# Attention and output projection: the merge weighed ahead of a pair's last values, and the projection's first column tile computed inside the last merge

## The chip, the cores and the metric

The kernel runs on one core of one Trainium2 chip. A core has five engines with a queue each: TensorE (PE in the profile; its weight loads are the row PEld), VectorE (DVE), ScalarE (ACT), GpSimd (POOL) and SyncE (SP), which here only issues DMAs. The metric is the device time of one execution in microseconds. The kernel before was timed in three runs: 2714.69, 2719.62 and 2720.20 us, so its median is 2719.62 us.

## What is computed

One layer of a decoder for 2048 prompt tokens and 64 sample tokens, with a model width of 1024. The first half of the mixer is attention with 8 heads of 64, in three patterns of window and dilation whose outputs are merged with weights from their softmax denominators. The second half is a gated linear attention. Both halves, side by side, go through the output projection `w_o`. A feed-forward part follows. Cut to what the change touches:

```python
PATTERNS = ((128, 1), (512, 4), (2048, 16))

def combine_patterns(results):
    outs = jnp.stack([o for o, _ in results], axis=0)
    lses = jnp.stack([l for _, l in results], axis=0)
    w = jax.nn.softmax(lses, axis=0)
    return jnp.sum(w[..., None] * outs, axis=0)

def prompt_attn(q, k, v):
    return combine_patterns([dilated_prompt(q, k, v, w, d) for w, d in PATTERNS])
...
mixed = jnp.concatenate([o_a.reshape(B, T, -1), o_b.reshape(B, T, -1)], axis=-1) @ w_o
x = x + rmsnorm(mixed, g_post_mix)
```

## The kernel before

**Stages.** `run` calls `sweeps` (projections and gated linear attention), `attention` (prompt attention), and `tail` (output projection, norms, feed-forward). The order in each engine's queue is not the order of the program: a planner simulates the engines and moves instructions that are ready ahead of others, and the code ties it down where it matters with `after(b, a)` (b is queued behind a on the same engine, without a wait) and `line`, which chains instructions that way one after the other.

**Attention.** The 8 heads are taken in four pairs (`pr` 0 to 3). A pair has three patterns, and a pattern four groups `g`. A group is cut into two units for the first two patterns and one for the third, so a pair has 20 units (`AtUnit`). A unit has three steps. `qk_` makes the scores of both heads on TensorE (L1880, tile `pas`), adds the mask and takes the row minimum of the negated scores on VectorE (L1885), and exponentiates on ScalarE (L1889). The minima and sums go into small tables `ML` (tile `aml`). `t` transposes the probabilities on TensorE (L1906, `pat`) and evicts them (`apt`, L63 on ScalarE, L65 on VectorE). `pv` multiplies them with the values (L1925, `pao`) and evicts the outputs unweighted into `OP` (`aop`, L65). Units wait in `fifo`: `pv` of a unit is issued two to three units behind its scores, and units are taken out in twos. For the second and third pattern GpSimd gathers the strided queries first (`at_gather`, L1134, `aqg`). PSUM has eight banks: four for scores (tag `as`), two for the transposes (`apt`), two for outputs (`ao`).

**Merge.** When a pair's last unit has been taken out of the fifo, `drain` makes a generator `at_merge` for it, and the loop over the next pair takes it forward by `next(pend)`, as often per group as the table `mst` says. The generator's first part weighs the patterns: 16 products on TensorE bring two of the `ML` tables into the order of the third (L1143 and L1146, `pam`), VectorE picks and reduces (L1152 to L1161, `atm`, `aw`), and some 15 small operations with one exponential on ScalarE (L1175) give the weights `aaw`. For pairs 0 to 2 the second step transposes `aaw` on TensorE (L1201, `pab`), sends it through DRAM (`awd`) so that it can be loaded spread over 64 rows (`awb`), and GpSimd then multiplies and adds the outputs (L1214 to L1221) and stores the merged rows to DRAM (`mixa`).

**Last merge.** For pair 3 nothing follows that would hide it, so it is done from PSUM, in four blocks `cb` of 128 columns by four residues. Of a block, each of the three patterns needs its weights spread (L1237 on ScalarE or L1239 on GpSimd, by the list `aa`), four transposes on TensorE (L1241, `pab`) and one multiplication on VectorE (L1242). Then two additions follow (L1245, L1247) and the store. The small operations of the weights are on GpSimd for this pair.

**Output projection.** It computes eight column tiles `m` for each of four token chunks `c` of 528 tokens. A column tile sums over eight input tiles `k`, in the order `WORD = (4, 5, 6, 7, 0, 1, 2, 3)`: 4 to 7 come from the linear attention (`mixb`), 0 to 3 from pairs 0 to 3 of the attention (`mixa`). Every operand is split into a high part (ScalarE, L70) and a low part (VectorE, L73), and three products with two halves of the tokens each are taken (L1439, `pbo`), so an input tile costs a column tile six products. `wo_pre` loads and splits the first column tile's weights and the input tiles 4, 5 and 6 during pair 3, in memory that no longer serves the attention. The other input tiles of chunk 0 (7, 0, 1, 2) are loaded and split by `wo_x(0)` at the start of `tail`, input tile 3 is split inside the last merge, straight from its result. `wo(0)` first takes column tiles 0, 1 and 2 through the input tiles 4 to 2, then adds input tile 3. The tail has its own PSUM pool of eight banks (`g1`).

## Time and profile before

| | |
|---|---|
| median of three runs | 2719.62 us (2714.69 to 2720.20) |
| the profiled execution | 2722.77 us, span 2721.0 us, mean granted clock 0.992 |
| attention, from first to last score and value product | about 765 to 1035 us of the span |
| last merge and start of the projection | about 1035 to 1062 us |
| TensorE busy in 1062 to 1252 us (rest of the projection) | 190.00 of 190 us |

All other numbers are read from one profiled execution. Its time is the span plus what lies around it, and it is 3.15 us above the median of the runs. A row of the timeline gives the start in us from the span's start, the busy time, the engine, the line of the kernel, the operation, output and inputs by tile name, shapes, and how many neighbouring instructions were put together; in brackets stands the idle time ahead of it and who ended it. A row of the waits gives who waited for whom. "Granted clock" is the share of TensorE's full clock that it was allowed.

### The profile page before, as it was taken

Reading aid. Unit: us, or ns where it says so; the run is one execution under the profiler, and the core shown is the slowest. Engines: PE = TensorE matmul, PEld = TensorE weight load, DVE = VectorE, ACT = ScalarE, POOL = GpSimd, SP = SyncE. Lnnn points to the kernel's source line nnn. Section 1 sums busy time; section 2 is a strip of 40 time slices with the busy share of each in tenths; the row PEclk is TensorE's granted clock in tenths of the full one; section 3 lists DMA queues with packets and bytes.
Section 4 is the critical chain, followed back from the end, with each engine's and each line's share of the span. In section 5 each row is a group of like instructions: output and inputs, shape, how many; then the busy total and the mean of one; then the engine's idle time right before and its main releaser. Section 6 shows DMA issues by size and latency. Waiting matters only on the chain.

```text
span 2721.0 us, 58225 instructions
## 1 busy us (share of the span) xinstructions
PE 2643.1 (97%) x22203; PEld 2518.3 (93%) x22203; DVE 1853.8 (68%) x4441; ACT 1270.2 (47%) x2961; POOL 373.6 (14%) x516
## 2 busy tenths in 40 slices
PE   8999999999999998999999999999999999999998
PEld 6888899878798887999999999999999999999998
DVE  7645645555457785468799899865776665766666
ACT  6535433333368883445555445433344332443333
POOL 2223120000045672011000020000110000200001
PEclk9999999999999998999999999999999999999999
DMA  8755536799776663376687589985798865976654
GB/s 321 255 176 179 186 131 211 268 331 369 272 263 191 192 173 109 129 260 251 244 286 288 196 314 333 350 294 198 256 330 289 282 228 203 336 248 216 221 184 164
DMA packets 288935, 661.67 MB, mean 243 GB/s; under 512 B 33344, under 2 KB 83136, under 8 KB 286608
## 3 DMA queue, kind: packets, MB, share of 16 engines
q1 hardware_dynamic: 260368, 588.97, 62.9%
q0 software_dynamic: 11296, 37.12, 3.7%
q10 hardware_dynamic: 16992, 31.86, 3.2%
q8 instruction: 175, 2.87, 0.4%
q14 instruction: 104, 0.85, 0.1%
HBM read 511.45 MB, written 146.37 MB: 242 GB/s over the span
## 4 chain that ended last, share of the span: by engine, by line
PE 79%; DVE 8%; DMA 6%; ACT 2%; issue 2%; POOL 1%; SPq 1%; DVEq 0%; ACTq 0%; POOLq 0%
PE pfd L92 17%; PE pv L399 9%; PE pq L92 8%; PE pfe L1636 8%; PE pfd L1636 8%; PE pfa L1636 7%; PE pbo L1439 7%; PE pfb L1636 4%; PE pas L1880 2%; DVE ws L73 2%; PE pao L1925 2%; PE pat L1906 2%; DMA raw<-in_xn 1%; DMA wr<-in_wd 1%; DMA ws<-d_wst 1%
## 5 line engine op out<-in xcount | busy, mean ns | idle before, releaser
L70 ACT ACTIVATE ws<-wr 128x512 fp32r<-128x512 f32 (+1 forms) x482 | 292.7, 616 | 423.7 <-PE pfd L92 160.9
L92 PE MATMUL pfd<-hh,ws 128*128 128x264 f32 x2816 | 470.2, 285 | 5.0 <-ACT ws L70 3.8
L73 DVE TENSOR_TENSOR ws<-wr,ws 128x512 fp32r<-128x512 f32 (+1 forms) x482 | 319.8, 669 | 127.5 <-ACT ws L70 116.1
L92 PEld LDWEIGHTS pfd<-hh,ws 128*128 128x128 f32 x2816 | 397.3, 188 | 6.5 <-ACT ws L70 4.8
L92 PE MATMUL pfd<-hl,ws 128*128 128x264 f32 x1408 | 298.6, 284 | 0.0
L1636 PE MATMUL pfe<-xh,ws 128*128 128x264 f32 x1496 | 290.5, 286 | 7.7 <-DVE u L1623 4.8
L1636 PE MATMUL pfa<-xh,ws 128*128 128x264 f32 x1496 | 289.8, 285 | 6.2 <-ACT ws L70 3.5
L1636 PE MATMUL pfd<-xh,ws 128*128 128x264 f32 x1408 | 288.9, 285 | 0.5 <-DVE gt L1623 0.3
L1636 PEld LDWEIGHTS pfe<-xh,ws 128*128 128x128 f32 x1496 | 236.4, 189 | 9.6 <-DVE u L1623 5.7
L1636 PEld LDWEIGHTS pfa<-xh,ws 128*128 128x128 f32 x1496 | 235.3, 188 | 8.3 <-ACT ws L70 4.6
L399 PE MATMUL pv<-wh,xh 128*128 128x256 f32 (+1 forms) x816 | 233.2, 286 | 2.2 <-DVE th L696 2.2
L1636 PEld LDWEIGHTS pfd<-xh,ws 128*128 128x128 f32 x1408 | 231.2, 189 | 0.9 <-DVE gt L1623 0.5
L399 PE MATMUL pv<-wl,xh 128*128 128x256 f32 (+1 forms) x816 | 231.3, 283 | 0.0
L399 PE MATMUL pv<-wh,xl 128*128 128x256 f32 (+1 forms) x816 | 231.2, 283 | 0.0
L92 PEld LDWEIGHTS pfd<-hl,ws 128*128 128x128 f32 x1408 | 223.6, 188 | 0.0
L1636 PE MATMUL pfd<-xl,ws 128*128 128x264 f32 x704 | 200.5, 285 | 0.0
L1665 DVE TENSOR_TENSOR acc<-acc,pfd 128x264 f32<-128x264 f32 x304 | 116.9, 424 | 115.9 <-PE pfd L92 115.2
L1889 ACT ACTIVATE ass<-ass,aml 128x256 f32<-128x256 f32 (+1 forms) x384 | 172.7, 453 | 46.1 <-DVE aml L1885 45.6
L92 PE MATMUL pq<-xh,wh 128*128 128x512 f32 (+2 forms) x480 | 173.2, 367 | 8.3 <-ACT xh L234 7.9
L1636 PE MATMUL pfe<-xl,ws 128*128 128x264 f32 x616 | 175.6, 285 | 0.0
L1636 PE MATMUL pfa<-xl,ws 128*128 128x264 f32 x616 | 175.0, 284 | 0.0
L92 PE MATMUL pq<-xh,wl 128*128 128x512 f32 (+2 forms) x480 | 173.0, 361 | 0.0
(334 smaller groups left out, 6277.3 us busy)
## 6 DMA issues: line engine op xcount, KB each, us to landing
ws<-d_wst SPq DMA_DIRECT2D x248, 512.0 KB, 5.4
wr<-in_wu SPq DMA_DIRECT2D x114, 512.0 KB, 4.8
d_wst<-ws SPq DMA_DIRECT2D x88, 512.0 KB, 3.6
wr<-in_wd SPq DMA_DIRECT2D x160, 256.0 KB, 3.5
wr<-in_wt SPq DMA_DIRECT2D x60, 512.0 KB, 8.0
wh<-d_wbs SPq DMA_DIRECT2D x35, 512.0 KB, 5.4
wl<-d_wbs SPq DMA_DIRECT2D x35, 512.0 KB, 5.4
skp<-in_ckt SPq DMA_DIRECT2D x16, 1024.0 KB, 9.0
```

Of the source, the lines that this page charges most:

```text
L70: h = nc.scalar.activation(hi, src, AF.Copy)
L73: return h, (nc.gpsimd if lo_eng == "p" else nc.vector).tensor_tensor(lo, src, hi.bitcast(F32), op=ALU.subtract)
L92: mm = nc.tensor.matmul(o, ww[:, k, :], xx[:, s0:s0 + n], start=(k == order[0] and i == 0), stop=(k == order[-1] and i == 2))
L399: mm = nc.tensor.matmul(ps[:m, :256], x[:, t0:t0 + m], w[:, k % 4, :], start=(k == 0 and i == 0), stop=(k == KT - 1 and i == 2))
L1439: self.lastmm = nc.tensor.matmul(o, ww[:, k, :], xx[:, s0:s0 + n], start=k == self.WORD[0] and i == 0, stop=k == self.WORD[-1] and i == 2)
L1636: self.lastmm = nc.tensor.matmul(bank[:, :H], w[:, ww, k, :], xx, start=new and k == 0 and j == 0, stop=k == 3 and j == 2, skip_group_chec ...
L1665: nc.vector.tensor_tensor(acc[m][:, s0:s0 + n], acc[m][:, s0:s0 + n], pz, op=ALU.add)
L1880: self.line(nc.tensor.matmul(ps[:, sc:sc + nk], lq, rk[z], start=(z == 0), stop=(z == 1)))
L1889: ex = nc.scalar.activation(ssb[:, sc:sc + nk], ssb[:, sc:sc + nk], AF.Exp, bias=self.ml[:, idx, h:h + 1], scale=-1.0, accum_out=self.ml[: ...
L1906: self.line(nc.tensor.transpose(ptp[:, len(tl), :], ssb[:, sc + 128 * j:sc + 128 * j + 128], L.ident))
L1925: self.line(nc.tensor.matmul(po[64 * h:64 * h + 64, blk, :], L.vq[self.base + kb][:, 64 * h:64 * h + 64], pt[:, j, :], start=st, stop=sp))
```

## The change

**The merge is made earlier.** In `drain`, when the last unit of a pair is the next to be taken out, the transposes of that unit are issued first if the fifo is being emptied, the merge is made and its first part is issued at once, ahead of the value products of the last two units. The table `mst` gives one step less in the second group. The `pam` products of pair 3 take their bank from the scores' tag, and the small operations of its weights go to VectorE.

**The last merge is interleaved with the projection.** `attention` now starts `wo(0)`. Four times it takes one step of the projection's column tile 0 (first input tiles 4 to 7, then 0, 1, 2), and one block of the merge. The blocks use only the `ao` banks for their transposes. Two of three spreads go to ScalarE and one to GpSimd. Both additions of a block go to GpSimd. The 16 columns of block 1 that chunk 0 needs are added on VectorE beforehand.

**Loads and buffers.** `wo_pre` loads the first weights in two halves, and then seven of the eight input tiles instead of three. The memory at the right side holds 16 split input tiles instead of 8 and no raw weights; four raw weight tiles and the split weights of column tiles 1 and 2 now lie at the left, behind 16 tiles that are placed first. The attention's PSUM pool stays open for the tail, whose banks go round the same eight by the tags `as`, `as`, `apt`, `ao`.

```diff
-    AB = dict(mst=((1, 1, 2, 1, 1, 1, 0, 1, 0, 0, 1, 1), (1, 1, 2, 1, 1, 1, 1, 1, 0, 1, 1, 1)),
+    AB = dict(mst=((1, 0, 2, 1, 1, 1, 0, 1, 0, 0, 1, 1), (1, 0, 2, 1, 1, 1, 1, 1, 0, 1, 1, 1)),
...
-            self.app = self.pool(ctx, "atp", bass.MemoryType.PSUM)
+            self.app = self.pool(self.tctx, "atp", bass.MemoryType.PSUM)
+            self.psum, self.bi = self, 0
...
                     un.t()
-                    un.pv()
-                    if un.last:
+                    if fifo and fifo[0].last:
+                        end = fifo[0]
+                        if not n:
+                            end.t()
                         for _ in pend or ():
                             pass
-                        pend = self.at_merge(un.pr, un.ML, un.OP)
+                        pend = self.at_merge(end.pr, end.ML, end.OP)
+                        next(pend)
+                    un.pv()
...
             drain(0)
+            self.wog = self.wo(0, self.xnext)
+            for _ in range(4):
+                next(self.wog)
+                next(pend)
             for _ in pend:
                 pass
...
-        pm = pp.tile([128, 512], F32, name=self.n("pam"), tag="ao", bufs=AB["po"])
+        pm = pp.tile([128, 512], F32, name=self.n("pam"), tag="as" if pr == 3 else "ao", bufs=AB["ps" if pr == 3 else "po"])
...
-        em, line = (nc.gpsimd, lambda x: x) if pr == 3 else (nc.vector, self.line)
+        em, line = nc.vector, (lambda x: x) if pr == 3 else self.line
...
-                if j in AB['aa']:
+                if (3 * cb + i) % 3 < 2:
                     nc.scalar.copy(ab, src)
...
                 for r in range(4):
-                    nc.tensor.transpose(pb[:, r, :], W[i][:, r, :], self.ident)
+                    tr = nc.tensor.transpose(pb[:, r, :], W[i][:, r, :], self.ident)
+                    if r == 0 and i == 0:
+                        self.after(tr, self.lastmm)
                 nc.vector.tensor_tensor(OP[i][:, :, sl], OP[i][:, :, sl], pb, op=ALU.mult)
...
+                nc.gpsimd.tensor_tensor(OP[1][:, :, sl], OP[0][:, :, sl], OP[1][:, :, sl], op=add)
+                nc.gpsimd.tensor_tensor(mo.rearrange("p (m r) -> p r m", r=4), OP[1][:, :, sl], OP[2][:, :, sl], op=add)
...
     def bank(self, name):
-        return self.psum.tile([128, 512], F32, name=self.n(name), tag="g1", bufs=8)
+        return self.tile([128, 512], F32, self.n(name))
+
+    def tile(self, shape, dt, name, tag=None, bufs=None):
+        tg, nb = (("as", "ps"), ("as", "ps"), ("apt", "ppt"), ("ao", "po"))[self.bi // 2 % 4]
+        self.bi += 1
+        return self.app.tile(shape, dt, name=name, tag=tg, bufs=self.AB[nb])
...
-        for k in self.WORD[:3]:
+        hi, lo = (self.slot("w", [128, 8, 128], F32R, n) for n in ("wh", "wl"))
+        for j in range(2):
+            ks = slice(4 * j, 4 * j + 4)
+            r = self.raw()[:, :512].rearrange("p (k c) -> p k c", k=4)
+            nc.sync.dma_start(r, a["wo"][0].rearrange("p (k c) -> p k c", k=8)[:, ks])
+            for i, e in zip(self.split(hi[:, ks], lo[:, ks], r, "v"), self.atl):
+                self.after(i, e)
+            yield
+        self.wow.append((hi, lo))
+        for k in self.WORD[:7]:
+            if k == 2:
+                yield
+                yield
...
-        for m in range(3 if c == 0 else 0):
-            part(m, self.WORD[:-1])
+        if c == 0:
+            for ks in (self.WORD[:4], *((k,) for k in self.WORD[4:-1])):
+                part(0, ks)
+                yield
+            for m in (1, 2):
+                part(m, self.WORD[:-1])
```

## The prediction

> **What bounds the kernel now.** I read the page first, then the waits of TensorE over the attention of pairs 1 to 3 and over the hand-over to the output projection (waiting engine, line, what it waited for: us in total, times, longest).

> ```profile
> PE 2643.1 (97%) x22203; PEld 2518.3 (93%) x22203; DVE 1853.8 (68%) x4441; ACT 1270.2 (47%) x2961; POOL 373.6 (14%) x516
> ```
> ```profile
> PE pab L1201 <- DVE aaw L1184: 5.8, 3, 1.9
> PE pas L1880 <- POOL aqg L1134: 2.1, 3, 1.1
> ```
> ```profile
> PE pab L1241 <- ACT awb L1237: 6.3, 1, 6.3
> PE pbo L1439 <- DVE aop L1242: 2.0, 1, 2.0
> PE pbo L1439 <- DVE xl L73: 1.8, 1, 1.8
> ```

> TensorE bounds the whole, so a change pays what it removes from TensorE's idle time or slow time, and nothing else. There are two such places. Each of the three ordinary merges stops TensorE once, 5.8 us together, because the transpose at L1201 needs the finished weights `aaw`. The last merge and the start of the projection stop it for 6.3 + 2.0 + 1.8 = 10.1 us. Both have a second price, which the windows show (columns: length, PE, PEld, DVE, ACT, POOL busy with counts, granted clock, DMA share, GB/s):

> ```profile
> 830.00:844.00 14.00, 12.10 (x132) 11.11 (x130) 13.64 (x60) 11.06 (x40) 0.00 (x0) 1.00 0.67 200
> 840.00:845.00 5.00, 2.83 (x24) 2.42 (x23) 4.30 (x23) 4.36 (x16) 0.00 (x0) 1.00 0.89 297
> 845.00:850.00 5.00, 5.00 (x47) 4.53 (x46) 2.52 (x10) 2.08 (x8) 2.70 (x3) 0.66 0.48 157
> ```
> ```profile
> 830.06 1.97 PE L1925 MATMUL pao<-apt,av 128*64 128x128 f32 x32
> ...
> 833.63 1.00 PE L1143 MATMUL pam<-aml,atab 128*128 128x64 f32 x8
> ...
> 845.42 3.38 PE L1925 MATMUL pao<-apt,av 128*64 128x128 f32 x32
> ```

> In the window with the idle TensorE is busy for 2.83 of 5 us, and in the next the granted clock is 0.66: the same 32 value products take 3.38 us instead of 1.97. So one stop costs 1.92 us of idle (5.8 over three) plus 3.38 - 1.97 = 1.4 us of slow clock, 3.3 us in all; three stops, 10.0 us.

> [...]

> **Part 1: ordinary merges weighed before the last values.** Before, the merge's first part was made only at the end of the next pair's fourth unit, and its `pam` products ran at 833.63, behind the value products of the old pair's last two units (from 830.06). After, it is made ahead of them, so `pam` moves about 833.63 - 830.06 = 3.6 us forward. Nothing is added on TensorE: `pam` and the 32 value products change places. The transpose at L1201 stays at its place in the order. The chain on VectorE that starts behind `pam` therefore has 3.6 us more, and only 1.92 were missing. What speaks against counting all of it is VectorE, busy for 13.64 of the 14 us from 830: the chain gets ahead only by passing evictions and score passes, which then come later themselves. They have room only behind the transpose, where VectorE is busy 2.52 us in 5. I take the idle as gone, 5.8 us. Of the slow clock I take less. GpSimd gathers the strided queries, and TensorE already waits 2.1 us for it (`aqg`, above) in the later pairs, so a faster TensorE meets that wait earlier. I count the clock's 1.4 us whole for one pair, half for the second, none for the third: 2.1. Part 1 is -7.9 us, between -10.0 (everything) and 0 (VectorE gives nothing back).

> **Part 2: the last merge.** Here are the chain of waits, TensorE's timeline, the windows of this stage and of the last pair ahead of it, and the groups of the stage 1035 to 1056:

> ```profile
> 1033.97 0.42 DVE atm L1152
> ...
> 1040.57 0.62 ACT awb L1237
> ...
> 1056.15 18.93 PE pbo L1439 x141
> ```
> ```profile
> 1033.86 1.09 PE L1925 MATMUL pao<-apt,av 128*64 128x128 f32 x14
> 1041.24 8.33 PE L1241 MATMUL pab<-c_ident,awb 128*128 128x128 f32 x48 [6.29 <-ACT awb L1237]
> ```
> ```profile
> 1041.00:1050.00 9.00, 8.52 (x49) 8.28 (x49) 7.16 (x12) 3.10 (x6) 6.92 (x10) 0.66 0.08 30
> 1057.00:1061.00 4.00, 4.00 (x23) 4.00 (x22) 4.00 (x5) 2.27 (x4) 0.00 (x0) 0.57 0.75 253
> 985.00:1000.00 15.00, 13.93 (x144) 12.12 (x140) 13.46 (x43) 14.14 (x51) 14.84 (x12) 1.00 0.81 197
> 1000.00:1020.00 20.00, 18.87 (x190) 17.90 (x189) 13.25 (x79) 18.90 (x80) 19.39 (x18) 0.91 0.31 95
> 1062.00:1252.00 190.00, 190.00 (x1572) 190.00 (x1571) 107.56 (x180) 81.03 (x170) 19.18 (x28) 1.00 0.59 203
> ```
> ```profile
> L1242 DVE TENSOR_TENSOR aop<-aop,pab 128x512 f32<-128x512 f32 x12 | 7.8, 684 | 2.8 <-PE pab L1241 2.8
> L1239 POOL TENSOR_SCALAR awb<-aaw 128x512 f32<-128x512 f32 x7 | 4.2, 616 | 1.4 <-PE pab L1241 1.4
> ...
> L1247 POOL TENSOR_TENSOR amo<-aop,aop 128x512 f32<-128x512 f32 x2 | 2.6, 1284 | 0.7 <-DVE aop L1245 0.5 <-DVE aop L1242 0.2
> L1249 POOL DMA_DIRECT2D d_mixa<-amo x4 | 2.2, 557 | 4.6 <-DVE amo L1247 4.0 <-DVE halo L1365 0.4 <-POOL amo L1247 0.3
> L70 ACT ACTIVATE xh<-br 128x528 fp32r<-128x528 f32 x4 | 2.2, 627 | 0.0
> ```

> What is lost before: 10.1 us idle, the clock in the transposes 9.0 x (1 - 0.66) = 3.1, the clock at 1057 4.0 x (1 - 0.57) = 1.7. Together 14.9 us.

> What is left after, counted from the end of the attention's value products (1033.86 + 1.09 = 1034.95). The chain from `atm` (1033.97) to the first spread weight (1040.57 + 0.62 = 1041.2) lasts 7.2 us. It starts earlier by the 18 value products that now follow `pam` instead of preceding it (18 x 1.97 / 32 = 1.1 us) and by the evictions between them, about 0.8 by estimate: 1.9. Eleven small operations go from GpSimd to VectorE, and three crossings between engines with them; three such operations in the two places:

> ```profile
> 843.67 0.44 DVE L1184 TENSOR_TENSOR aaw<-aaw,amm 128x32 f32<-128x32 f32 x3
> ```
> ```profile
> 1040.05 0.71 POOL L1184 TENSOR_TENSOR aaw<-aaw,amm 128x32 f32<-128x32 f32 x3 [0.47 <-DVE amm L1182]
> ```

> Eleven save 11 x (0.71 - 0.44) / 3 = 1.0, and with the crossings I estimate 1.2 us. So the weight is there 6.3 - 1.9 - 1.2 = 3.2 us behind the value products. TensorE fills this with 24 products of column tile 0, at 18.93 / 141 = 0.134 us each 3.2 us. The stop is covered; were the cover gone (input tiles 4 to 7 not split in time), 3.2 us would come back. Then come four blocks. VectorE has 12 multiplications (7.8), one 512-wide split and small pieces (estimate 1.2), and perhaps part of the two weight splits (estimate 0.5): 9.5 us. TensorE's own work there is 48 transposes, 8.33 x 0.66 = 5.5 us at full clock, and 18 products, 2.4 us: 7.9. So 1.6 us are lost, and I add 0.5 for the entry and 1.4 for GpSimd, whose part per block (spread 0.62, two additions 2 x 1.28, issue 0.56: 3.7 us) is longer than VectorE's. Loss after: 3.5. Part 2 is 3.5 - 14.9 = -11.4 us; bounds of the loss 1 (VectorE alone) and 10 (rival three), so -13.9 to -4.9.

> The waits for `aop` and `xl` go too: the banks stay in the attention's pool, and tiles 7, 0, 1, 2 are split before the merge. Late next are tile 3 and the weights of column tiles 1 and 2. Tile 3 is needed behind 84 products (11.3 us), the weights at the end of the blocks. Their 512 KB loads can start only when the K strips of pair 3 are free, but that is ahead of the last transposes.

> **Part 3: what moves forward.** Four more input splits now run inside pair 3: four loads on SP's queue, 4 x 0.627 = 2.5 us on ScalarE, about as much on VectorE. ScalarE is busy 14.14 of 15 and 18.90 of 20 us there, so they are not free; TensorE however idles there for GpSimd (14.84 of 15, 19.39 of 20). I count +1.5, between 0 and +3. The load of tile 2 is the risky one:

> ```profile
> 1023.17 0.35 SPq L1411 DMA_DIRECT2D br<-d_mixa  x1
> ```

> It waits until GpSimd has stored the second block of pair 2, and what is queued behind it on SP waits too. Its split stands before the last transposes on ScalarE or behind them; wrongly placed it holds up the eviction of the last scores' transposes (in the 3 above). From 1062 to 1252 TensorE is busy for 190.00 of 190 us, so a lead won here is carried on. The rings of the tail keep their number of buffers, and the banks still go round eight; I cost these at nothing, covered by that same full stretch.

> **A rule against the change.** VectorE's split of a weight tile beside GpSimd and without it:

> ```profile
> 989.22 1.91 DVE L73 TENSOR_TENSOR wl<-wr,wh 128x1024 fp32r<-128x1024 f32 x1
> ```
> ```profile
> 1057.87 4.62 DVE L73 TENSOR_TENSOR wl<-wr,wh 128x1024 fp32r<-128x1024 f32 x4
> ```

> With GpSimd at work one takes 1.91 us, alone 4.62 / 4 = 1.16. The change puts eight additions on GpSimd beside VectorE's work. By these rows the two weight splits could lose 2 x 0.75 = 1.5 us, inside the bounds above. [...]

> **Sum.** -7.9 - 11.4 + 1.5 = -17.8 us; I take -17, because the splits may cost some of the pairs' gain twice. The profiled execution took 2722.8 us with a span of 2721.0, the median of the runs is 2719.6, lowest 2714.7: the profiled one lies 3.2 us above the median. From the profiled one 2705.8, from the median 2702.6. I forecast the median: 2703.

> **The rivals.** *VectorE is full (0.22).* The merge chain starts earlier but ends no earlier, or the clock stays low. For it: 13.64 of 14 us. Against: 3.6 us of head start for 1.92 missing. Part 1 falls to about -2: 2719.6 - 2 - 11.4 + 1.5 = 2707.7. [...]

> *GpSimd paces the last merge (0.12).* If its spreads stay behind its additions, a block takes 3.7 us and some 0.5 for TensorE and VectorE's answer, four take 16.8 instead of 9.5: Part 2 falls to 3.5 + 7.3 - 14.9 = -4.1, so 2719.6 - 7.9 - 4.1 + 1.5 = 2709.1. Against is GpSimd's own order in this stage, where the planner put spreads of later blocks ahead of the first addition:

> ```profile
> 1040.72 2.37 POOL L1239 TENSOR_SCALAR awb<-aaw 128x512 f32<-128x512 f32 x4
> ...
> 1045.94 1.29 POOL L1247 TENSOR_TENSOR amo<-aop,aop 128x512 f32<-128x512 f32 x1 [0.25 <-DVE aop L1242]
> ```

> *The change does nothing in the order (0.06).* The planner moves `pam` and the projection back behind the values: some -4 is left, 2716.

> *Slower: `pam` holds an output bank (0.05).* In the ordinary pairs `pam` now takes one of two banks that the value products need. If VectorE, full there, frees it late, TensorE stops ahead of the last unit's values. Up to 1.92 us of stop per pair this only replaces the old one. From about 5 us per pair (5 + 1.4 - 3.3 = 3.1 more, 9.3 over three pairs) it eats the 11.4 - 1.5 us of the rest, and at 8 us per pair, with rival three beside it: 3 x 6.1 - 4.1 + 1.5 = +15.7, 2735. VectorE's two reads of `pam` are 0.42 us each, so this needs a long queue ahead of them.

> **How the numbers follow.** The forecast has 0.55; its own range is 2698 to 2709 (bounds of the two parts). The cases reach 2713 with 1 in 10 beyond, below 2696 lie all bounds at their best: 2696 to 2713. A measurement of this kernel can tell about 0.2%, 5.4 us. Below 2714.2 lie the forecast and the first two rivals but for their ends: 0.87. Within 0.2%: 0.08. Slower: 0.05.

> **What would show it.** Right: no wait of TensorE at the ordinary transposes and a granted clock of 1.00 behind them; `pbo` products between the last merge's transposes; the first wait of the last merge under 1 us; `xl` and the banks gone from TensorE's waits. Wrong: the 1.9 us waits stay or turn into waits for `pao` banks; waits on GpSimd's `awb` in the blocks; a longer `aqg` wait; a late weight split behind the blocks.

## The result and the profile after

| kernel | median | range | runs |
|---|---|---|---|
| before | 2719.62 us | 2714.69 to 2720.20 | 5 |
| after | 2730.64 us | 2728.86 to 2737.67 | 5 |

The changed kernel is slower: ratio 1.0050, 95% interval 1.0034 to 1.0066. The prediction was 2703 us and faster. The profiled execution of after took 2728.86 us, with a span of 2727.1 us and a mean granted clock of 0.989 (before 0.992).

**The ordinary merges.** The waits of TensorE over pairs 1 to 3 (820 to 985 us), in after:

```profile
PE pao L1963 <- DVE apt L65: 6.9, 4, 3.3
PE pam L1152 <- DVE aop L65: 1.0, 1, 1.0
PE pas L1918 <- POOL aqg L1143: 0.6, 1, 0.6
```

The 5.8 us at the transpose are gone, as forecast. Yet the list adds up to 8.5 us. In before it was 8.1: 5.8 at the transpose and 2.3 in three more groups:

```profile
PE pas L1880 <- POOL aqg L1134: 0.9, 2, 0.6
PE pat L1906 <- DVE apt L65: 0.8, 3, 0.3
PE pao L1925 <- ACT apt L63: 0.6, 1, 0.6
```

The idle time has moved. VectorE's timeline at the merges in pairs 2 and 3, both in after, shows the first reason, and GpSimd's timeline in pair 2 shows the stores that VectorE waits for:

```profile
896.70 0.42 DVE L1161 TENSOR_TENSOR atm<-pam,atab 128x256 f32<-128x256 f32 x1 [5.34 <-DMA d_mixa<-amo]
```
```profile
964.17 0.42 DVE L1161 TENSOR_TENSOR atm<-pam,atab 128x256 f32<-128x256 f32 x1 [4.52 <-DMA d_mixa<-amo]
```
```profile
890.00 1.27 POOL L1228 TENSOR_TENSOR aop<-aop,awb 128x512 f32<-128x512 f32 x1 [2.30 <-DMA awb<-d_awd]
891.35 1.29 POOL L1230 TENSOR_TENSOR amo<-aop,aop 128x512 f32<-128x512 f32 x1
892.93 0.58 POOL L1232 DMA_DIRECT2D d_mixa<-amo  x1 [0.30 <-POOL amo L1230]
```

The weighing's table `atm` lies in one of two buffers with the tag `amo`. The other users of that tag are the merged rows, which the older pair's merge is still making on GpSimd and storing. Moved forward, the weighing meets those stores: VectorE stands at `atm` for 5.3 and 4.5 us. The next `apt` copies in its order run only behind `atm` (in pair 2 at 897.38), and TensorE stops for them. A low clock follows (columns as in the prediction):

```profile
895.00:900.00 5.00, 1.47 (x10) 1.07 (x12) 3.30 (x10) 0.00 (x0) 4.00 (x4) 0.70 0.69 207
900.00:905.00 5.00, 5.00 (x34) 4.67 (x30) 4.60 (x19) 3.29 (x11) 0.00 (x0) 0.62 0.69 197
```

In pair 1 no older merge exists. There `atm` waits for `pam` alone (2.1 us), and no such stop follows.

**The last merge.** The `pbo` blocks run between the transposes, and no wait of TensorE there is over 0.7 us. But when the blocks are done TensorE has nothing (its timeline, then SP's):

```profile
1052.87 1.32 PE L1249 MATMUL pab<-c_ident,awb 128*128 128x128 f32 x8
1064.23 0.81 PE L1469 MATMUL pbo<-xh,wh 128*128 128x264 f32 x2 [10.05 <-ACT wh L70]
```
```profile
1029.91 4.19 SPq L1510 DMA_DIRECT2D bx<-in_xn  x3
1055.62 1.27 SPq L1446 DMA_DIRECT2D wx<-d_mixb  x3
1056.94 2.04 SPq L1297 DMA_DIRECT2D wr<-in_wo  x4
```

The raw weights of the next column tiles (`wr`) were issued at 1056.94. From 1034.1 SP stood at `wx`, the first input tiles of the next chunk, whose buffers come free only after GpSimd's last additions. In the program the weights come first, but the planner put `wx` ahead. The chain of waits goes through it:

```profile
1054.33 1.28 POOL aop L1268
1055.61 0.02 issue
1055.62 0.33 SPq L1446
...
1056.94 6.16 DMA wr<-in_wo
1063.10 0.02 issue
1063.13 1.06 ACT wh L70
```

**The end.** From the start of the last `pfd` product to the end of the span before took 14.8 us, after 18.4. The wait there, after and then before:

```profile
PE pn L126 <- DVE fssq L1307: 5.2, 1, 5.2
```
```profile
PE pn L126 <- DVE fssq L1293: 2.5, 2, 1.7
```

**Where the time went.** The table gives stretches in us between starts of the same products, read from the timelines. "s192" is the score product (`pas`) with that number, counted from 0; a pair has 192. "v" is the last value product (`pao`), "p126" a projection product (`pbo`) with that number, which is where three column tiles have had seven input tiles, "d" the last `pfd`. "Before again" is experiment 10 below, the same kernel a second time. The last four columns are experiments 1, 5, 9 and 6. Each column is one execution; that of experiment 1 was the fastest of its runs, that of experiment 5 the slowest.

| stretch | before | before again | after | weights first | + table | + tile 2 | early pairs + table |
|---|---|---|---|---|---|---|---|
| s192 to s264 (merge in pair 1) | 33.2 | 31.6 | 30.8 | 30.8 | 30.8 | 30.8 | 30.8 |
| s384 to s456 (merge in pair 2) | 32.6 | 33.8 | 35.4 | 35.3 | 32.1 | 33.4 | 33.1 |
| s456 to s576 | 33.6 | 33.7 | 32.9 | 33.0 | 35.9 | 33.9 | 35.8 |
| s576 to s648 (merge in pair 3) | 32.5 | 30.9 | 35.0 | 34.8 | 30.6 | 30.7 | 31.8 |
| s648 to v (rest of pair 3) | 48.3 | 50.6 | 50.4 | 50.6 | 52.6 | 47.4 | 51.1 |
| v to p126 (last merge, column tiles) | 36.0 | 34.1 | 37.0 | 28.8 | 28.9 | 27.3 | 37.3 |
| d to the end | 14.8 | 14.7 | 18.4 | 18.5 | 18.5 | 18.5 | 14.7 |

Against the mean of the two traces of before, after loses 2.1 and 3.3 us at the merges in pairs 2 and 3, 1.0 in the rest of pair 3, 2.0 from v to p126 and 3.7 at the end. It gains 1.6 at the merge in pair 1 and 0.8 behind the one in pair 2. Together that is +9.7 us. The spans of the traces differ by less, 6.0 us, because after takes 3.9 us less from p126 to d; there the traces of all kernels lie between 1631 and 1639 us, and why is not shown. The medians of the runs differ by 11.0 us: the profiled execution of before was slower than its median, that of after faster.

### The profile page after: what moved, and what is told of

It reads as the page before. It is cut to its first block, busy times and chain, and to the rows that moved or that the text cites. A ratio compares the mean times of both kernels' runs of the same rounds, so it can differ in the third digit from the quotient of the medians.

```text
span 2727.1 us, 58244 instructions
## 1 busy us (share of the span) xinstructions
PE 2646.7 (97%) x22203; PEld 2519.7 (92%) x22203; DVE 1852.6 (68%) x4449; ACT 1273.9 (47%) x2965; POOL 381.6 (14%) x508
## 4 chain that ended last, share of the span: by engine, by line
PE 78%; DMA 8%; DVE 6%; POOL 3%; issue 2%; ACT 2%; SPq 0%; DVEq 0%; ACTq 0%; POOLq 0%
PE pfd L92 17%; PE pv L399 9%; PE pfe L1674 8%; PE pfa L1674 8%; PE pfd L1674 8%; PE pq L92 7%; PE pbo L1469 7%; PE pfb L1674 4%; DMA raw<-in_xn 2%; DVE ws L73 1%; PE pas L1918 1%; PE pao L1963 1%; PE pat L1944 1%; POOL aqg L1143 1%; POOL aop L1223 1%
## 5 line engine op out<-in xcount | busy, mean ns | idle before, releaser
L70 ACT ACTIVATE ws<-wr 128x512 fp32r<-128x512 f32 (+1 forms) x482 | 293.3, 616 | 411.5 <-PE pfd L92 148.6
L92 PE MATMUL pfd<-hh,ws 128*128 128x264 f32 x2816 | 476.4, 286 | 5.7 <-DVE up L1661 4.2
L73 DVE TENSOR_TENSOR ws<-wr,ws 128x512 fp32r<-128x512 f32 (+1 forms) x482 | 319.6, 668 | 122.0 <-ACT ws L70 114.0
L92 PE MATMUL pfd<-hl,ws 128*128 128x264 f32 x1408 | 305.9, 285 | 0.4 <-DVE hl L73 0.4
```

Source lines behind the costliest of these rows:

```text
L70: h = nc.scalar.activation(hi, src, AF.Copy)
L73: return h, (nc.gpsimd if lo_eng == "p" else nc.vector).tensor_tensor(lo, src, hi.bitcast(F32), op=ALU.subtract)
L92: mm = nc.tensor.matmul(o, ww[:, k, :], xx[:, s0:s0 + n], start=(k == order[0] and i == 0), stop=(k == order[-1] and i == 2))
```

## The experiments

Theories at the start: (A) the weights' loads stand behind the next chunk's inputs on SP; (B) `atm` in a shared buffer stops VectorE in pairs 2 and 3. The rival to B: VectorE or GpSimd has no room for the merge moved forward, wherever the table lies. A ratio is to the kernel before on the same chip, with its 95% interval.

**1. The weights first.** The next chunk's first input load (`d`) is bound behind the weights' loads on SP.

```diff
+        self.wrd = self.nc.sync.dma_start(raw[:, k0:nk], src.rearrange("p (k c) -> p k c", k=nk)[:, k0:])
...
+                if c == 1 and k == 4:
+                    self.after(d, self.wrd)
```

> Changed kernel, with one order tied: the loads of the next column tiles' weights go ahead of the next chunk's first input load on SP's queue. Theory (SP's order): the 10.0 us wait for the split weights at 1054 us is the loads standing behind an input load that waits for GpSimd's last additions; the wait falls below 2 us, the products from the 43rd to the 127th of the projection take about 12 us instead of 25, and the time is 10 to 14 us below the changed kernel's, 2717 to 2721 (about 1.000 of the kernel before). Rival (memory): the weights' own place is not free before the merge ends, the wait stays, 2728 to 2733.

2720.51 us, ratio 1.0007 (0.9997 to 1.0017), so 10 us less than after by the medians, as expected. SP's queue and TensorE's waits from 1036 to 1070:

```profile
1027.91 4.20 SPq L1512 DMA_DIRECT2D bx<-in_xn  x3
1032.16 2.29 SPq L1297 DMA_DIRECT2D wr<-in_wo  x4
1053.61 1.28 SPq L1446 DMA_DIRECT2D wx<-d_mixb  x3
```
```profile
PE pbo L1471 <- DVE wl L73: 1.1, 1, 1.1
PE pab L1249 <- ACT xh L70: 0.7, 1, 0.7
PE pbo L1471 <- ACT wh L70: 0.7, 1, 0.7
```

A is shown: issued 25 us earlier the weights are there, and of the 10 us 1.8 are left (1.1 and 0.7 for `wl` and `wh`), the split itself, which stands behind the blocks on ScalarE and VectorE. From v to p126 it takes 28.8 us instead of 37.0.

**2. The table in a score buffer**, with the weights first, and without them in the early pairs alone (experiments 2 and 4 below share the edit).

```diff
-        if pr == 3:
+        if True:
             tm = self.aq[1].tile([128, 512], F32, name=self.n("atm"), tag="ass", bufs=AB["s"])
```

> As the run before, and the merge's table of pairs 0 to 2 takes one of the score buffers instead of a buffer that the old pair's stores still read. Theory (shared buffer): VectorE's waits of 5 us for the stores in the second and third pair go, each of these merges gains about 2.4 us against the kernel before like the first one does, instead of losing 2.6: 8 to 11 us more, 2707 to 2712 (0.996 to 0.997). Rival (VectorE full): nothing beyond the run before, 2717 to 2721.

2720.94 us, ratio 1.0011 (0.9999 to 1.0024). Nothing was gained, but it doesn't test B: the planner, which had to wait for a score buffer, put `atm` behind eight score passes, and both the old wait and a new one for the bank that `pam` holds came up (820 to 985 us):

```profile
PE pab L1210 <- DVE aaw L1193: 5.3, 3, 1.8
PE pao L1965 <- DVE aop L65: 4.6, 3, 1.9
```

**3. The early pairs alone**: the kernel before with the new `mst` and the early weighing for pairs 0 to 2; last merge, buffers and loads as before.

```diff
+                    if fifo and fifo[0].last and n:
+                        end = fifo[0]
+                        for _ in pend or ():
+                            pass
+                        pend = self.at_merge(end.pr, end.ML, end.OP)
+                        next(pend)
                     un.pv()
-                    if un.last:
+                    if un.last and not n:
```

> Kernel before, with the merges of pairs 0 to 2 weighed ahead of the last values and nothing else. Theory (shared buffer): first pair -2.4 us, second and third +2.6 each, together about +3 us, 2720 to 2724 (1.000 to 1.002). Rival (VectorE full): about 0 in each of the three. The forecast's own step would have been -8 us.

2727.65 us, ratio 1.0029 (1.0015 to 1.0043). This part, forecast at -7.9 us, costs about 8 by the ratio, more than either theory gave it.

**4. The same with the score buffer.**

> As the run before, with the merge's table in one of the score buffers. Theory: the early weighing by itself is worth -2.4 us in each of the three pairs and more where the slow clock goes, -6 to -9 us, 2711 to 2714 (0.997 to 0.998). Rival (VectorE full): as the run before.

2730.37 us, ratio 1.0038 (1.0026 to 1.0051), spoilt by the late `atm` like experiment 2.

**5. The table in a weight buffer.** The spread weights `awb` have two buffers that are free long before. Otherwise this is the weights-first kernel, and the order of all queues stays but for one reduction.

```diff
-            tm = p.tile([128, 512], F32, name=self.n("atm"), tag="amo", bufs=2)
+            tm = p.tile([128, 2, 4, 128], F32, name=self.n("atm"), tag="awb2", bufs=2).rearrange(...)[:, :512]
```

> The weights-first kernel, with the weighing table `atm` of the ordinary merges in a buffer of the broadcast weights `awb` (free by then) in place of one of the two `amo` buffers that the older merge is still storing from. The order on every engine stays that of the weights-first kernel but for one reduction. Theory (the shared buffer is why pairs 2 and 3 lost): VectorE's wait of 5.3 us at `atm` is gone at pairs 2 and 3, their stretches go from 2.7 and 2.3 us over the kernel before to some 2.4 under it, as pair 1's did, and the stretch behind pair 3's merge loses 1 to 3 of its 4 us; in all 10 to 13 us less than the weights-first kernel's 2720.5: 2708 to 2711. Rival (GpSimd is late with the older merge anyway): the wait passes to the next `amo` buffer, `awt`, or to the gathered queries, and the time stays within 3 us of 2720. Rival (the weighing's VectorE work itself is what delays the exponentials' `apt` copies): no wait on a DMA at `atm`, but PE's 3.3 us waits for `apt` stay: 2718 to 2722.

2716.65 us, ratio 0.9982 (0.9973 to 0.9992), some 7 us less than experiment 1 by the ratios; forecast were 10 to 13. VectorE no longer stands at `atm`, and the merges in pairs 2 and 3 take 32.1 and 30.6 us instead of 35.3 and 34.8. B is shown for these two stretches: the wait at `atm` came from the shared buffer. But TensorE now stops elsewhere (ScalarE's and TensorE's waits, 1015 to 1036):

```profile
ACT xh L70 <- DMA br<-d_mixa: 3.4, 1, 3.4
```
```profile
PE pao L1965 <- ACT apt L63: 3.5, 1, 3.5
PE pas L1920 <- POOL aqg L1143: 1.7, 1, 1.7
```

That is the risk named in Part 3 of the prediction: the split of tile 2 waits for its load, the load for GpSimd's store, and the copy of `apt` stands behind the split.

**6. The early pairs alone, with that buffer.**

> The kernel before with the ordinary merges weighed early, as in the run of the early pairs alone (2727.65), and `atm` in the buffer of `awb`. Nothing of the last merge or of the weights' loads is changed. Theory of the shared buffer: pairs 1, 2 and 3 each gain some 2.4 us on the kernel before, 2711 to 2716; what the prediction gave this part alone was 7.9 us less than before, 2711. Rival (GpSimd late, or VectorE's work): 2724 to 2730 as without the other buffer.

2727.09 us, ratio 1.0029 (1.0017 to 1.0041): not better than experiment 3, where 2711 to 2716 was expected; it lies in the rival's range. TensorE's waits from 820 to 985 us, and the window 920 to 950:

```profile
PE pao L1931 <- DVE apt L65: 3.5, 2, 1.9
PE pas L1886 <- POOL aqg L1140: 2.5, 4, 1.3
PE pam L1149 <- DVE aop L65: 1.0, 1, 1.0
```
```profile
920.00:950.00 30.00, 27.48 (x291) 25.06 (x288) 19.66 (x102) 25.59 (x109) 29.50 (x26) 1.00 0.43 104
```

The shared buffer was only the first thing in the way. What TensorE no longer loses at the transpose it loses for `apt` copies behind the weighing on VectorE (1.9 and 1.6 us, at the merges in pairs 2 and 3) and for gathered queries: 2.5 us where before lost 0.9. In the window TensorE is busy 27.48 of 30 us, where before has 29.07, and GpSimd 29.50.

**7. The last merge alone**: experiment 1 with the ordinary merges where the kernel before has them.

```diff
-                    if fifo and fifo[0].last:
+                    if fifo and fifo[0].last and fifo[0].pr == 3:
...
                     un.pv()
+                    if un.last and un.pr < 3:
+                        for _ in pend or ():
+                            pass
+                        pend = self.at_merge(un.pr, un.ML, un.OP)
```

> The weights-first kernel with the merges of pairs 0 to 2 weighed where the kernel before weighs them (behind the pair's last values, with its number of merge steps); only the last merge is weighed early, with the blocks of column tile 0 inside it. The weights-first kernel took 7.2 us less than the kernel before from the last value product to the 126th product of the output projection. Theory (the parts add): those 7.2 us less, plus 0.4 to 1.5 us for the four splits inside pair 3, so 2711 to 2713. If instead the 4 us that the stretch ahead of the last merge lost come from the four splits and not from the older merge's lag, 2715 to 2717.

2718.08 us, ratio 0.9995 (0.9984 to 1.0006). Neither range was met. Its trace has the 28.9 us from v to p126, and also the 18.5 us at the end.

**8. The last merge and the first.** As 7, with `fifo[0].pr in (0, 3)` and `un.pr in (1, 2)`.

> As the last merge alone, and the merge of pair 0 weighed early too, the only ordinary one that has no older merge still storing behind it. Theory of the shared buffer: pair 1's stretch gains the 2.4 us that it gained in every kernel with early weighing and the shared table, the pairs behind it stay as before: 2.4 us under the last merge alone, 2708 to 2711. Rival (early weighing costs VectorE as much as it saves PE): the same as the last merge alone.

2715.66 us, ratio 0.9984 (0.9974 to 0.9994), 2.4 us under experiment 7 by the medians. That is the expected difference, but the time is over the expected 2708 to 2711, and the intervals overlap. The merge in pair 1 takes 30.8 us instead of 33.0.

**9. Tile 2's split behind the copies.** Experiment 5 with the split of tile 2 bound behind the last `apt` copies.

```diff
-            for i, e in zip(self.split(hi, lo, r, "v"), self.atl):
+            for i, e in zip(self.split(hi, lo, r, "v"), (self.atc[True], self.atc[False]) if k == 2 else self.atl):
```

> The kernel with the table in the weight buffer, with one more edit: the split of activation tile 2 is bound behind the last copies of `apt` on ScalarE and VectorE, where that kernel has it ahead of them. There ScalarE's split waited 3.44 us for the load of tile 2 (pair 2's results, which GpSimd was still storing), the copy of `apt` stood behind it, and PE stopped 3.45 us at `pao`. Theory (the stop was that split's place in ScalarE's queue): no wait of PE for `apt` over 1 us behind 1015, and 3 to 4 us less: 2712 to 2714. Rival (the wait passes to the last merge's exponential or its first weights, which now stand behind the same split, or to block 7's products, which need tile 2): PE stops 2 us or more between 1030 and 1050, and the time stays within 2 us of 2717.

2713.84 us, ratio 0.9983 (0.9973 to 0.9994). The median lies in the expected range, but the ratio is that of experiment 5 (0.9982), so no gain in the time is shown. The stop of 3.5 us is gone from the trace, and the last value products come 5.2 us earlier after s648. In experiment 11, whose order there is the same, they come only 2.1 us earlier (50.5 us instead of 52.6). The longest wait of TensorE from 1015 to 1036 is now 0.4 us:

```profile
PE pab L1249 <- DVE aop L1252: 0.4, 1, 0.4
```

**10. The kernel before again**, unchanged.

> The kernel before, unchanged, for a second trace of it: how far do its stretches differ between two executions with nothing changed? The stretches of the merges and of the last merge (the starts of the same products in both traces) should agree within 0.5 us if they are set by the order of the work; the stretch behind the 126th product of the output projection, 1650 us, may differ by the 4 us by which the changed kernels' traces differed there.

The merges don't agree within 0.5 us: 31.6, 33.8 and 30.9 instead of 33.2, 32.6 and 32.5. The order and the three stops of 1.9 us at the transposes are the same; the waits of `pat` for `apt` are 0.9 us longer in the second trace. What differs most is the granted clock: in the 10 us from 840, 905 and 970 us it is 0.83, 0.83 and 0.83 in the first trace, and 1.00, 0.83 and 1.00 in the second. The last section takes it up. The rest of pair 3 differs by 2.3 us here, and by 3.1 between experiments 9 and 11, which have the same order up to the end. So a single difference of up to some 3 us between two traces is not proof of an effect. From p126 to the last `pfd` the traces differ by 2.9 us.

**11. The order of the end too.** Experiment 9, with the columns of the last half chunk bound one behind the other, and `pn` and `pb` where the kernel before had them.

```diff
-                self.gemm([(pd[:, :n], s0, n)], wds[m], hs, G)
+                self.gemm([(pd[:, :n], s0, n)], wds[m], hs, G, prev=(0, {2: self.pnmm, 4: self.pbmm}.get(m, self.lastmm)) if z else None)
```

> The kernel with tile 2's split behind the copies, and the end of the program put back in the order of the kernel before: in the last chunk's second half each down-projection column is bound behind the one before it, with the norm's products `pn` and `pb` ahead of its third and fifth. In every kernel with the changed last merge the planner put a column's products behind `pb` and the last sums of squares behind eight scaling passes on VectorE, and from the last `pfd` product to the end took 18.45 us, where the kernel before and those with its last merge took 14.7. Theory: that stretch falls to 14.7 us and the time by 3.7: 2709 to 2711. Rival (the order before makes PE wait for `pn` and `pb` in the middle of the columns): the gain at the end is paid back ahead of it, within 1 us of 2713.8.

2717.14 us, ratio 0.9978 (0.9966 to 0.9990). From the last `pfd` to the end it takes 14.6 us, and the waits are those of before:

```profile
PE pn L126 <- DVE fssq L1307: 2.5, 2, 1.6
```

So the 3.7 us at the end came from the planner's order. The median doesn't show them: it lies 3.3 us above that of experiment 9 and over both expected ranges, the ratio is lower, and the intervals of both ratios overlap. What in the change turned the planner there was not tried; the kernels with the last merge of before don't have it.

**12. The last merge alone, with the order of the end.**

> The kernel with the last merge alone (ordinary merges as before, weights first), and the same binding at the end. That kernel was 2.4 us under the kernel before by the medians, where its stretch from the last value product to the 126th product of the output projection was 7.2 us shorter; the theory is that the end's 3.7 us and the four splits' 0.7 us took the rest. Then this one is 6 us under the kernel before: 2712 to 2714. Rival (the last merge is worth less in most executions than in the profiled one): 2715 to 2717.

2715.74 us, ratio 0.9990 (0.9981 to 0.9999). That is the rival's range: the last merge is worth 2.7 us by the ratio and 4 by the medians, although its stretch from v to p126 is 6 us shorter than the mean of the two traces of before and the end is as before. The two traces of before are of executions 3 and 4 us above its medians; where the other executions are faster isn't shown.

**13 to 15. GpSimd relieved.** In all three the ordinary merges leave out one of the three patterns' multiplications, so the output is not the attention's.

```diff
-                for i in (1, 0):
+                for i in (1,):
                     line(nc.gpsimd.tensor_tensor(OP[i][:, :, sl], OP[i][:, :, sl], W[:, i], op=ALU.mult))
```

> The kernel before with one thing left out: the ordinary merges don't multiply the first pattern's values by their weights (four GpSimd operations of 1.29 us in each of three merges, so the output isn't the attention's). It is the base for the next two. TensorE waited 0.9 us for GpSimd's gathered queries `aqg` between 914 and 955 in the kernel before; those waits should go: 2716 to 2720.

> The kernel with the early pairs alone and the table in the weight buffer, with the same multiplications left out. With them it took 7.9 us more than the kernel before, though TensorE no longer stops at the ordinary transposes; its waits for `aqg` between 914 and 955 had grown from 0.9 to 2.5 us, with GpSimd busy 9.7 to 9.9 of 10 us. Theory (GpSimd sets the pace of pairs 2 and 3, so what TensorE gains at the merge it gives back at the gathers): with GpSimd relieved the early weighing gains what the prediction gave it, 5 to 8 us less than the base with the same omission, 2709 to 2714, and the `aqg` waits of that stretch are under 0.5 us. Rival (VectorE pays for it): at the base or up to 8 us above it.

> The kernel with all four repairs (weights first, table in the weight buffer, tile 2's split behind the copies, the order of the end), with the same multiplications left out. With them it was 2.6 us under the kernel before by the medians. Theory of GpSimd's pace: 12 to 15 us less than the base with the same omission (5 to 8 from the pairs, 7 from the last merge): 2702 to 2707. Rival: 3 to 6 us under that base, 2712 to 2716.

The base: 2719.52 us, ratio 0.9998 (0.9989 to 1.0007), so less work on GpSimd doesn't help the kernel before. The early pairs: 2718.49, ratio 0.9993 (0.9981 to 1.0004), where they were at 1.0029 without the relief. The repaired change: 2717.12, ratio 0.9988 (0.9978 to 0.9999). In the early pairs' trace no wait for `aqg` is left between 820 and 985 us, and the window of experiment 6 reads:

```profile
920.00:950.00 30.00, 29.90 (x323) 28.31 (x322) 23.41 (x126) 28.34 (x121) 28.11 (x26) 1.00 0.48 132
```

TensorE is busy 29.90 of 30 us instead of 27.48. The base with the same omission has 29.90 there too, against 29.07 in before, and is no faster for it. So with less work on GpSimd the loss of 8 us is gone. That GpSimd's pace was the cause is likely, but not shown, because the omission also moved the planner's order. In pair 2 it put `pam` ahead of the last 14 of the 32 value products, and the weighing on VectorE ahead of score passes (TensorE, experiment 6, then the early pairs relieved):

```profile
884.19 2.32 PE L1931 MATMUL pao<-apt,av 128*64 128x128 f32 x32
888.33 1.00 PE L1149 MATMUL pam<-aml,atab 128*128 128x64 f32 x8
```
```profile
881.40 1.30 PE L1931 MATMUL pao<-apt,av 128*64 128x128 f32 x18
883.73 1.10 PE L1149 MATMUL pam<-aml,atab 128*128 128x64 f32 x8 [1.02 <-DVE aop L65]
885.65 1.09 PE L1931 MATMUL pao<-apt,av 128*64 128x128 f32 x14
```

No run has the relief with the old order, which would tell the two apart. Nor does the early weighing lose 8 us wherever GpSimd is not relieved: beside the new last merge, experiment 5 takes no more than experiment 7, which lacks it (1.4 us less by the medians, 3.5 by the ratios). A loss of 8 us appears only beside the last merge of before. There, in experiment 6, TensorE waits 4.1 us for the projection's split `xl`, where the two traces of before wait 1.8 and 0.3. Why the parts don't add up stays open.

The second half of the theory falls: even with GpSimd relieved the early weighing gains 1 us on its base, not 5 to 8, and the repaired change 2.4, not 12 to 15. The early pairs lie at their base within the noise, as the rival has it, by which VectorE pays; the repaired change lies just outside its rival's 3 to 6 us.

## Why the prediction was wrong

**The slowdown: Part 2, "Late next are tile 3 and the weights of column tiles 1 and 2 … Their 512 KB loads can start only when the K strips of pair 3 are free, but that is ahead of the last transposes."** This step failed, and it is what makes the changed kernel slower. I asked when the memory is free, not what stands ahead of the loads on SP. From 1034.1 the loads stood 22.8 us behind `wx`, which waited for GpSimd. I counted nothing; it was a wait of 10.0 us, and one edit of the order on SP takes 10 us back. Without it the change is level with before (ratio 1.0007), not 17 us faster. By the table the largest part of what is still missing is then Part 1: from s192 to s648 experiment 1 takes 2.9 us more than the mean of before, where -7.9 was forecast. "A late weight split behind the blocks" stands in the prediction as a sign that it would be wrong.

**The rest of Part 2.** The early weight, the cover of 24 products and the blocks came as forecast: with the weights first, no wait before the last transposes is over 0.7 us. The size was off. Work of 20.7 us (48 transposes at the forecast's 5.5, 126 products at 190/1572 us) leaves a loss of 8.1 us in the 28.8, where the prediction had 3.5. Of the difference of 4.6, 1.8 are the waits for the split of column tile 1 and 1.7 the half clock behind them; 1.1 are not told apart (weights first: window, and VectorE's splits):

```profile
1055.00:1060.00 5.00, 5.00 (x30) 5.00 (x30) 3.81 (x3) 1.92 (x3) 4.05 (x5) 0.66 0.91 278
```
```profile
1052.86 4.04 DVE L73 TENSOR_TENSOR wl<-wr,wh 128x1024 fp32r<-128x1024 f32 x2
1058.08 2.36 DVE L73 TENSOR_TENSOR wl<-wr,wh 128x1024 fp32r<-128x1024 f32 x2 [1.19 <-POOL amo L1269]
```

Both come from the weights again. Beside GpSimd's last additions two splits take 4.04 us, behind them 2.36: what the prediction put against the change by its two rows, 1.5 us inside its bounds, is 1.7 us at this place. GpSimd's spreads did not pace the last merge: no wait for `awb` stands in TensorE's list.

**Part 1.** "The chain gets ahead only by passing evictions and score passes" was right, and what followed from it was not. The prediction looked for room on VectorE behind the transpose. It did not ask which buffer the moved chain writes to, and who holds it. The head start was larger than the forecast 3.6 us: counted from the start of each pair's scores, `pam` runs 8.0 us earlier in pair 1 and 5.5 us in pairs 2 and 3, because it passes score products too. So moved, `atm` ran into the older pair's stores in pairs 2 and 3. With that away, the idle in experiment 6 still only changes its place, to `apt` copies behind the weighing and to GpSimd's gathers. The prediction named both (VectorE full, the `aqg` wait met earlier), but took the second off the clock's share alone. Only in pair 1 the gain is there in every trace (30.8 us in every kernel that weighs early without a score buffer): 1.6 us against the mean of the two traces of before, 2.4 against the profiled one, where 3.3 was forecast. A bank that `pam` holds cost 1.0 us once, not the 5 per pair of the slower rival. The rival that came nearest is "VectorE is full", but its 2 us of gain are a loss of 8 in experiment 3.

**The slow clock as part of a stop's price.** The prediction gave every stop 1.92 us of idle and 1.4 us of slow clock. In the one execution that I had, half clock followed each of the three stops: 0.50 for 3.41 us from 845.78, 910.63 and 975.49. In the second trace of before it follows only one of the three (0.83 from 905 to 915 us, 1.00 from 840 to 850 and from 970 to 980).

**Part 3.** The four splits were given +1.5, 0 to 3. Against the mean of the two traces of before, the rest of pair 3 takes 0.4 us less with the last merge alone (49.1 against 49.5), and 3.1 more in experiment 5, where tile 2's split stands ahead of a copy. The named risk was real as a stop of 3.5 us in one trace; what it costs in the time is not shown.

**What was left out.** "The rings of the tail keep their number of buffers, and the banks still go round eight; I cost these at nothing." What this left out is the planner, which ordered the last half chunk otherwise: 3.7 us in the trace, 1600 us behind the change.

**The range.** 2698 to 2709 holds only one of the two parts at its bad bound. With both (0 and -4.9, and +1.5) the sum is 2716, beyond 2713 already, and in the runs both parts failed together.

**What the best version is worth.** With all four repairs (experiment 11) the change is faster than both kernels: ratio 0.9978 to before, 6 us by the ratio and 2.6 by the medians. The forecast was 17 us.

## What to carry to other kernels

When work is moved forward, list for each instruction not only its inputs but the buffer it writes and the older work that still holds it; and for each load, what stands ahead of it in its queue and what that waits for. A stop that one engine loses can come back at the next engine in the loop, so look for slack in the stretch that counts: GpSimd, 14% busy over the span, was 98% busy in the 30 us in which TensorE waited for it (experiment 6). An edit that relieves one engine can also move the planner's order, so compare the queues before the gain is put down to the relief. Bind the few orders on which a plan rests, far from the edit too, since a planner may choose others.

## What the runs showed of the hardware

```profile
842.37:845.78 3.41, 1.52 (x15) 1.41 (x17) 2.65 (x17) 2.49 (x9) 0.61 (x2) 1.00 0.98 350
845.78:849.19 3.41, 3.41 (x32) 3.08 (x29) 1.09 (x7) 1.83 (x8) 2.09 (x2) 0.50 0.40 118
```
```profile
839.22:842.63 3.41, 1.76 (x14) 1.32 (x12) 3.31 (x19) 3.16 (x12) 0.00 (x0) 1.00 0.92 258
842.63:846.05 3.42, 2.91 (x41) 2.77 (x41) 2.12 (x12) 2.51 (x10) 2.00 (x3) 1.00 0.84 307
```

In the first the whole stop of 1.92 us falls into one step: TensorE is busy 1.52 of 3.41 us, and the next step has the clock at 0.50. In the second the same stop lies across two steps, which are busy 1.76 and 2.91 us, and the clock stays at 1.00. I divided the 17 traces of this case into their steps between 780 and 2650 us. Of the steps at full clock, half clock followed in 54 of the 55 with TensorE busy under 45%, in 28 of 45 between 45 and 55%, in 2 of 22 between 55 and 60%, in 5 of 566 between 60 and 95%, and in none of 8485 above; in the profiled executions of before and after alone in 8 of 8, 3 of 3, none of 2, 1 of 66 and none of 995. What decides between 45 and 55% is not shown. So here a stop of 1.9 us costs 1.9 us, or by estimate 3.6 (1.92 + 3.41 / 2) where a step of half clock follows it, and the two traces of before, of one kernel, differ in that.

**It may be part of the scatter.** The stretches of half clock within the span of one trace add up to between 28 us (experiment 9, mean clock 0.995) and 59 us (after, 0.989), with 11.5 of them at the end of the span in before and 14.2 in after; half the difference, the most that it can cost at a clock of 0.50, is 15 us. In the runs of experiment 9 those below 2712 us have mean clocks of 0.993 to 0.996, those above 2719 us 0.992. That the clock sets these times is not shown: the two traces of before have 46 and 52 us of half clock (mean clocks 0.992 and 0.990) and spans of 2721.0 and 2721.2 us.
